# Conv branch of a decoder layer: one 512-column product for the high weights, a bank for each unit

## The chip, the cores and the metric

The kernel runs on one core of one Trainium2 chip. The metric is the device time of one execution in microseconds; the time of a kernel is the median of its runs.

## The reference

One decoder layer on 256 tokens of width 1024, in float32: gated token mixers in parallel, then a feed-forward block, each followed by a LayerNorm. Cut to what matters here:

```python
proj = x @ w_in          # q | k | v | B | C | h | gates, 1024 -> 5120 columns
q, k = apply_partial_rope(q, cos, sin), apply_partial_rope(k, cos, sin)
y_att = moba_attention(q, k, v) @ w_attn_out       # 256 tokens: one block, plain causal attention
y_cnv = (gate_b * causal_dwconv(gate_c * h_in, conv_w_mix)) @ w_conv_out
mix = (g_att * y_att + g_cnv * y_cnv) @ w_o
x = layer_norm(DEEPNORM_ALPHA * x + mix, ln1_g, ln1_b)
u = causal_dwconv(x @ w_up, conv_w_ffn)
f = (silu(u[..., :D_FF]) * u[..., D_FF:]) @ w_down
x = layer_norm(DEEPNORM_ALPHA * x + f, ln2_g, ln2_b)
```

B, C and h have 512 columns each (the conv branch); the gates have 2048.

## The kernel before

**Products in three passes.** To keep float32 accuracy, every operand is split into a high part (rounded to the format that TensorE multiplies) and a low part (the rest). A product is then high x high, high x low and low x high, summed in PSUM. x is kept split and transposed in `xT`, eight k-tiles of 128 rows, each with 256 high columns and then 256 low columns (`xh` and `xl` are views of them). Weights come by DMA as raw chunks of 1 MB, two *units* of work in each, through three buffers (`RAW_BUFS`), queued on SP. `split` makes the high part `wh` on ScalarE and the low part `wl` on VectorE (`hl_split`, L213 to L215); nine buffers of each hold them (`HL_BUFS`).

**Units and steps.** A unit of the conv branch or of the gates is 128 output columns of `w_in`: eight k-tiles of 128x128 weights. The order of the conv units is h, c, b for the first 256 channels (`pr` 0) and then for the second (`pr` 1), two units each (`e` 0 and 1), twelve in all; sixteen gate units follow. Each unit is a step: `ahead(u)` queues the splits up to unit u+4 (`LA`), then TensorE's products are queued, then `run(u)` queues what was put down for that step with `at`. Every engine works off its queue in this order. Counted from the first h unit as step 0 (`C0`), attention is put down beside the conv units for each pair of heads p: `scores` at step 4+3p, `masked` (row maxima, VectorE) one step later, `exps` (ScalarE) two and `normalize` (VectorE) three steps later; `probs_T` at step 9+4p, the splits of the transposed probabilities `probs_hl` at 10+4p and 11+4p, `attend` at 12+4p, and `attend_hl` (from the bank of `attend` into `aT`, ScalarE and VectorE) at 13+4p.

**PSUM.** There are eight banks: four in the pool `acc` (the projections) and four in the pool `ps` (scores, transposes, attention outputs), each handed out in turn. A bank is handed out again once all that read it is done.

**Two forms of a unit.** `unit_cols` (L305 to L313) takes for each k-tile three products of 256 columns: wh with xh, wh with xl, wl with xh, all into the same 256 columns of a bank. The conv units use it, and the two units of one name share a bank, 256 columns each. `unit_cols_wide` (L315 to L323) takes for each k-tile one product of wh with all 512 columns of `xT` (L321), and afterwards eight products of wl with the high columns into the first half of the bank (L323). The gates use it: the two halves of a gate's bank are added by `gate_sum` (ScalarE copies one half to SBUF in L577, VectorE adds the other in L578).

**The conv work.** `conv1` copies h out of its bank (L532, ScalarE) and multiplies c from its bank with it (L535, VectorE); `conv2` applies the three taps (L542 on ScalarE, L545 four times on VectorE); `conv3` multiplies b from its bank (L551) and splits the result into `yT`, which is used after the gates. They stand at the first b unit of their `pr`, one and two steps later. `scratch` hands out SBUF buffers of one tag in turn, six of them.

Of the kernel before, what the change touches and what calls it, by code (L numbers as in the profile page):

```python
# [12 lines left out]
AF = mybir.ActivationFunctionType  # L13
ALU = mybir.AluOpType

P = 128
S = 256
# [35 lines left out]
OFF_B, OFF_C, OFF_H, OFF_G = 3 * AW, 3 * AW + CW, 3 * AW + 2 * CW, 3 * AW + 3 * CW  # L53
# [84 lines left out]
def layer_kernel(ctx: ExitStack, tc: tile.TileContext, x, wpack, cpack, ln1_g, ln1_b, ln2_g, ln2_b, out):  # L138
    nc = tc.nc
# [10 lines left out]
    def acc_bank(name):  # L150
        return psum.tile([P, 512], F32, tag="acc", name=name)

    def ps_bank(name):
        return ps_pool.tile([P, 512], F32, tag="ps", name=name)

    def scratch(shape, name, bufs=None, tag="scr"):
        return tmp.tile(shape, F32, tag=tag, name=name, bufs=bufs or 6)
# [5 lines left out]
    chunks, plan_units, U = plan()  # L163
# [49 lines left out]
    def hl_split(h, l, src, eng=None):  # L213
        nc.scalar.activation(h, src, AF.Copy)  # L214
        (eng or nc.vector).tensor_tensor(l, src, h.bitcast(F32), op=ALU.subtract)  # L215
# [38 lines left out]
    xT = big.tile([P, KT, 2, S], F32R, tag="xT", name="xT")  # L254
    xh, xl = xT[:, :, 0], xT[:, :, 1]
# [49 lines left out]
    def unit_cols(u, o, bh, bl, n0=0):  # L305

        un = units[u]
        nk = un["shape"][0]
        for k in range(nk):
            wh, wl = un["h"][:, k, n0:n0 + P], un["l"][:, k, n0:n0 + P]  # L310
            nc.tensor.matmul(o, wh, bh[:, k, :], start=k == 0, stop=False)  # L311
            nc.tensor.matmul(o, wh, bl[:, k, :], start=False, stop=False)  # L312
            nc.tensor.matmul(o, wl, bh[:, k, :], start=False, stop=k == nk - 1)  # L313

    def unit_cols_wide(u, bank, b):  # L315


        un = units[u]
        nk = un["h"].shape[1]
        for k in range(nk):  # L320
            nc.tensor.matmul(bank, un["h"][:, k, :], b[:, k].rearrange("p a s -> p (a s)"), start=k == 0, stop=False)  # L321
        for k in range(nk):
            nc.tensor.matmul(bank[:, 0:S], un["l"][:, k, :], b[:, k, 0], start=False, stop=k == nk - 1)  # L323
# [4 lines left out]
    def ahead(u):  # L328
        for v in range(cur["u"], u + LA + 1):
            split(v)  # L330
        cur["u"] = max(cur["u"], u + LA + 1)
# [102 lines left out]
    def at(u, f, *a):  # L434
        after.setdefault(u, []).append((f, a))

    def run(u):
        for f, a in after.pop(u, []):
            f(*a)
# [14 lines left out]
    for p in range(4):  # L454
        s = C0 + 4 + 3 * p
# [4 lines left out]
        s = C0 + 9 + 4 * p  # L460
# [66 lines left out]

    CB = {}

    def conv1(pr):  # L530
        h = scratch([P, 2, S], f"ch{pr}")
        nc.scalar.activation(h, CB["h", pr], AF.Copy)  # L532
        z = scratch([P, 2, S + 2], f"z{pr}", tag="z", bufs=1)
        nc.vector.memset(z[:, :, 0:2], 0.0)
        nc.vector.tensor_tensor(z[:, :, 2:S + 2], CB["c", pr], h, op=ALU.mult)  # L535
        CB["z", pr] = z

    def conv2(pr):
# [9 lines left out]

    def conv3(pr):
        t = CB["t", pr]  # L550
        nc.vector.tensor_tensor(t, CB["b", pr], t, op=ALU.mult)  # L551
        hl_split(yT[:, 0, 2 * pr:2 * pr + 2, :], yT[:, 1, 2 * pr:2 * pr + 2, :], t)

    for pr in range(2):
        at(U[(OFF_B, pr)], conv1, pr)
        at(U[(OFF_B, pr)] + 1, conv2, pr)
        at(U[(OFF_B, pr)] + 2, conv3, pr)
        for nm, off in (("h", OFF_H), ("c", OFF_C), ("b", OFF_B)):
            bank = acc_bank(f"{nm}{pr}")
            CB[nm, pr] = bank.rearrange("p (e t) -> p e t", e=2)  # L560
            for e in range(2):
                u = U[(off, pr)] + e
                ahead(u)
                unit_cols(u, bank[:, e * 256:(e + 1) * 256], xh, xl)
                run(u)


# [16 lines left out]
    for j in range(16):  # L584
        u = U[("g", 0)] + j
# [27 lines left out]
    for half in range(2):  # L613
        for e in range(2):
            ua, uc = U[("ao", half)] + e, U[("co", half)] + e
            for n in range(2):
# [4 lines left out]
                bank = ps_bank(f"y{i}")  # L621
# [327 lines left out]
```

## Time and profile before

| | |
|---|---|
| median of 3 runs | 370.72 us (370.24 to 373.15) |
| the profiled execution, its own time | 370.11 us |
| its span in the profile | 368.3 us |
| granted TensorE clock, mean | 0.993 |
| TensorE busy | 359.3 us, 2122 products |
| VectorE busy | 291.9 us |
| ScalarE busy | 218.5 us |
| stage of the conv units | 37.75 to 77.89 us |
| stage of the gate units | 77.89 to about 129 us |

The profile is of one execution. Times are from the start of its span in microseconds; the span leaves out some 2 us of the execution's time. Engines: PE is TensorE's product, PEld its weight load, DVE is VectorE, ACT is ScalarE. A row of a timeline has the start, the duration, the engine, the line of the kernel, the operation, `out<-in` and the shapes, and in brackets the idle time just before it and what ended that. Products are pipelined, so their durations overlap, and the distance from one start to the next is what a product costs. A row of a group has the count, the busy time, the mean duration of one in ns, and the idle time before them. A line can be that of a helper: most splits stand under L214 and L215.

### The profile page before, as it was taken

Reading aid. Unit: us, or ns where it says so; the run is one execution under the profiler, and the core shown is the slowest. Engines: PE = TensorE matmul, PEld = TensorE weight load, DVE = VectorE, ACT = ScalarE, POOL = GpSimd, SP = SyncE. Lnnn points to the kernel's source line nnn. Section 1 sums busy time; section 2 is a strip of 40 time slices with the busy share of each in tenths; the row PEclk is TensorE's granted clock in tenths of the full one; section 3 lists DMA queues with packets and bytes.
Section 4 is the critical chain, followed back from the end, with each engine's and each line's share of the span. In section 5 each row is a group of like instructions: output and inputs, shape, how many; then the busy total and the mean of one; then the engine's idle time right before and its main releaser. Section 6 shows DMA issues by size and latency. Waiting matters only on the chain.

```text
span 368.3 us, 5515 instructions
## 1 busy us (share of the span) xinstructions
PE 359.3 (98%) x2122; PEld 317.3 (86%) x2122; DVE 291.9 (79%) x499; ACT 218.5 (59%) x365; POOL 9.3 (3%) x27
## 2 busy tenths in 40 slices
PE   8999999999999999999999999999999999999991
PEld 8888999998888899988888888888888888888891
DVE  4786968788586579869759898987888697899784
ACT  3766568568787645634266676675666566576300
POOL 2000000000000000102100000000000000000012
PEclk9999999999999999999999999999999999999997
DMA  7959653633555554586250935448274545562011
GB/s 273 332 210 356 216 222 116 230 114 116 229 201 164 207 197 169 187 362 222 122 219 12 340 122 223 163 182 322 65 299 132 212 149 204 219 235 109 1 57 57
DMA packets 11385, 69.63 MB, mean 189 GB/s; under 512 B 1248, under 2 KB 1888, under 8 KB 4320
## 3 DMA queue, kind: packets, MB, share of 16 engines
q1 hardware_dynamic: 10784, 67.20, 49.9%
q0 software_dynamic: 576, 2.10, 1.7%
q8 instruction: 16, 0.26, 0.3%
q14 instruction: 9, 0.07, 0.1%
HBM read 68.24 MB, written 1.05 MB: 188 GB/s over the span
## 4 chain that ended last, share of the span: by engine, by line
PE 98%; DVE 1%; issue 0%; DVEq 0%
PE pb L321 20%; PE pb L323 10%; PE g L321 8%; PE d L292 5%; PE d L293 5%; PE d L294 5%; PE g L323 4%; PE q L493 3%; PE k L493 3%; PE v L493 3%; PE y L313 2%; PE y L312 2%; PE y L311 2%; PE o L293 2%; PE o L292 2%; PE o L294 2%
## 5 line engine op out<-in xcount | busy, mean ns | idle before, releaser
L215 DVE TENSOR_TENSOR wl<-raw,wh 128x1024 fp32r<-128x1024 f32 (+1 forms) x70 | 77.0, 1123 | 16.6 <-ACT wh L214 16.0
L197 DVE TENSOR_TENSOR wl<-raw,wh 128x1024 fp32r<-128x1024 f32 x58 | 70.8, 1222 | 16.3 <-ACT wh L192 15.7
L321 PE MATMUL pb<-x1T,wh 128*128 128x512 f32 x320 | 79.8, 391 | 0.0
L214 ACT ACTIVATE wh<-raw 128x1024 fp32r<-128x1024 f32 (+1 forms) x70 | 66.1, 973 | 16.6 <-DMA raw<-in_wpack 11.0
L192 ACT ACTIVATE wh<-raw 128x1024 fp32r<-128x1024 f32 x58 | 60.9, 1054 | 18.5 <-DMA raw<-in_wpack 18.4
L321 PEld LDWEIGHTS pb<-x1T,wh 128*128 128x128 f32 x320 | 58.5, 188 | 11.1
L323 PEld LDWEIGHTS pb<-x1T,wl 128*128 128x128 f32 x320 | 43.7, 190 | 3.1
L323 PE MATMUL pb<-x1T,wl 128*128 128x256 f32 x320 | 44.6, 282 | 0.0
L321 PE MATMUL g<-xT,wh 128*128 128x512 f32 x128 | 32.3, 394 | 0.0
L292 PE MATMUL d<-wh,f 128*128 128x512 f32 x80 | 31.3, 391 | 0.0
L293 PE MATMUL d<-wl,f 128*128 128x512 f32 x80 | 31.3, 391 | 0.0
L294 PE MATMUL d<-wh,f 128*128 128x512 f32 x80 | 31.1, 389 | 0.0
L321 PEld LDWEIGHTS g<-xT,wh 128*128 128x128 f32 x128 | 23.0, 189 | 4.2
L709 ACT ACTIVATE fb<-pb 128x512 f32<-128x512 f32 x20 | 11.9, 596 | 24.5 <-PE pb L323 23.9
L727 DVE SCALAR_TENSOR_TENSOR fc<-fb,consts,fc 128x254 f32<-128x254 f32 x40 | 19.4, 484 | 1.4
L725 DVE SCALAR_TENSOR_TENSOR fc<-fb,consts,fc 128x255 f32<-128x255 f32 x40 | 19.2, 479 | 0.0
L323 PEld LDWEIGHTS g<-xT,wl 128*128 128x128 f32 x128 | 17.5, 190 | 1.3
L719 ACT ACTIVATE fc<-fb,consts 128x256 f32<-128x256 f32 x40 | 18.0, 497 | 0.3 <-DVE fb L713 0.3
L713 DVE TENSOR_TENSOR fb<-pb,fb 128x512 f32<-128x512 f32 x20 | 13.8, 688 | 5.4 <-ACT fb L709 5.1
L323 PE MATMUL g<-xT,wl 128*128 128x256 f32 x128 | 17.9, 282 | 0.0
L294 PEld LDWEIGHTS d<-wh,f 128*128 128x128 f32 x80 | 15.0, 188 | 3.2
L292 PEld LDWEIGHTS d<-wh,f 128*128 128x128 f32 x80 | 15.1, 188 | 2.7
(184 smaller groups left out, 676.6 us busy)
## 6 DMA issues: line engine op xcount, KB each, us to landing
raw<-in_wpack SPq DMA_DIRECT2D x55, 1024.0 KB, 4.9
raw<-in_wpack SPq DMA_DIRECT2D x6, 896.0 KB, 6.1
xr<-in_x SPq DMA_DIRECT2D x1, 1024.0 KB, 7.0
ln<-in_ln_g POOLq DMA_DIRECT2D x2, 512.0 KB, 5.4
ln<-in_ln_b POOLq DMA_DIRECT2D x2, 512.0 KB, 6.0
raw<-in_wpack SPq DMA_DIRECT2D x3, 256.0 KB, 3.1
raw<-in_wpack SPq DMA_DIRECT2D x1, 512.0 KB, 6.0
out<-x SPq DMA_DIRECT2D x2, 256.0 KB, 2.0
```

What stands on the lines that cost most here:

```text
L192: nc.scalar.activation(units[u]["h"], raw_of(u), AF.Copy)
L197: nc.vector.tensor_tensor(units[u]["l"], raw_of(u), units[u]["h"].bitcast(F32), op=ALU.subtract)
L214: nc.scalar.activation(h, src, AF.Copy)
L215: (eng or nc.vector).tensor_tensor(l, src, h.bitcast(F32), op=ALU.subtract)
L292: nc.tensor.matmul(o, ah, bh, start=start, stop=False)
L293: nc.tensor.matmul(o, ah, bl, start=False, stop=False)
L294: nc.tensor.matmul(o, al, bh, start=False, stop=stop)
L321: nc.tensor.matmul(bank, un["h"][:, k, :], b[:, k].rearrange("p a s -> p (a s)"), start=k == 0, stop=False)
L323: nc.tensor.matmul(bank[:, 0:S], un["l"][:, k, :], b[:, k, 0], start=False, stop=k == nk - 1)
L493: nc.tensor.matmul(banks[m][t], (xl if p == 2 else xh)[:, k, t * P:(t + 1) * P], wl if p == 1 else wh, start=k == 0 and p == 0, stop=k == ...
L725: nc.vector.scalar_tensor_tensor(c[:, 1:S], pb[:, a * S:a * S + S - 1], w_ffn(1, j), c[:, 1:S], op0=ALU.mult, op1=ALU.add)
L727: nc.vector.scalar_tensor_tensor(c[:, 2:S], pb[:, a * S:a * S + S - 2], w_ffn(0, j), c[:, 2:S], op0=ALU.mult, op1=ALU.add)
```

## The change

The conv units take the wide form, and each has a bank of its own, so that twelve banks are handed out in this stage where six were. A new function `conv_sum` adds the halves of a bank on the way out, into an SBUF tile that two units of a name share; it stands one step after its unit. `conv1` and `conv3` read h, c and b from these tiles, the copy of h in `conv1` is gone, and `conv1`, `conv2` and `conv3` stand one step later than before.

```diff
+    def conv_sum(nm, pr, e):
+
+        if e == 0:
+            CB["s", nm, pr] = scratch([P, 2, S], f"c{nm}{pr}")
+        s = CB["s", nm, pr][:, e]
+        bank = CB.pop((nm, pr, e))
+        nc.scalar.activation(s, bank[:, S:2 * S], AF.Copy)
+        nc.vector.tensor_tensor(s, bank[:, 0:S], s, op=ALU.add)
+
     def conv1(pr):
-        h = scratch([P, 2, S], f"ch{pr}")
-        nc.scalar.activation(h, CB["h", pr], AF.Copy)
         z = scratch([P, 2, S + 2], f"z{pr}", tag="z", bufs=1)
         nc.vector.memset(z[:, :, 0:2], 0.0)
-        nc.vector.tensor_tensor(z[:, :, 2:S + 2], CB["c", pr], h, op=ALU.mult)
+        nc.vector.tensor_tensor(z[:, :, 2:S + 2], CB["s", "c", pr], CB["s", "h", pr], op=ALU.mult)
         CB["z", pr] = z
...
-        nc.vector.tensor_tensor(t, CB["b", pr], t, op=ALU.mult)
+        nc.vector.tensor_tensor(t, CB["s", "b", pr], t, op=ALU.mult)
         hl_split(yT[:, 0, 2 * pr:2 * pr + 2, :], yT[:, 1, 2 * pr:2 * pr + 2, :], t)
 
     for pr in range(2):
-        at(U[(OFF_B, pr)], conv1, pr)
-        at(U[(OFF_B, pr)] + 1, conv2, pr)
-        at(U[(OFF_B, pr)] + 2, conv3, pr)
         for nm, off in (("h", OFF_H), ("c", OFF_C), ("b", OFF_B)):
-            bank = acc_bank(f"{nm}{pr}")
-            CB[nm, pr] = bank.rearrange("p (e t) -> p e t", e=2)
+            for e in range(2):
+                at(U[(off, pr)] + e + 1, conv_sum, nm, pr, e)
+        at(U[(OFF_B, pr)] + 1, conv1, pr)
+        at(U[(OFF_B, pr)] + 2, conv2, pr)
+        at(U[(OFF_B, pr)] + 3, conv3, pr)
+        for nm, off in (("h", OFF_H), ("c", OFF_C), ("b", OFF_B)):
             for e in range(2):
                 u = U[(off, pr)] + e
                 ahead(u)
-                unit_cols(u, bank[:, e * 256:(e + 1) * 256], xh, xl)
+                CB[nm, pr, e] = acc_bank(f"{nm}{pr}{e}")
+                unit_cols_wide(u, CB[nm, pr, e], xT)
                 run(u)
```

## The prediction

> **What bounds the kernel now.** I read the page first, then busy time by stage, then the timelines of TensorE, VectorE and ScalarE around the conv units, and last the groups kept apart by shape.
>
> ```profile
> span 368.3 us, 5515 instructions
> ...
> PE 359.3 (98%) x2122; PEld 317.3 (86%) x2122; DVE 291.9 (79%) x499; ACT 218.5 (59%) x365; POOL 9.3 (3%) x27
> ...
> PE 98%; DVE 1%; issue 0%; DVEq 0%
> ```
>
> The last row is the chain of work that ended last: 98% of it is TensorE following itself. Whatever shortens TensorE's stream shortens the kernel, unless another engine then ends last somewhere. For the stage of the change:
>
> ```profile
> 37.50:77.80 40.30, 40.30 (x348) 39.43 (x347) 33.41 (x79) 26.45 (x51) 0.00 (x0) 1.00 0.53 186
> ```
>
> The columns are span, PE, PEld, DVE, ACT, POOL, clock, DMA. TensorE never pauses here, its weight loads fill 39.43 of 40.30 us, the granted clock is 1.00. VectorE is busy 33.41 us: 6.9 us of slack in the stage, not spread evenly. So there are two questions: how much shorter does TensorE's stream get, and does the added work on VectorE and ScalarE stay hidden.
>
> **TensorE's term.** A conv unit is 24 products of 256 columns, each with its own weight load. A gate unit already has the new form: 8 products of 512 columns, then 8 of 256.
>
> ```profile
> 57.81 0.28 PE L311 MATMUL h<-xT,wh 128*128 128x256 f32 x1
> ...
> 60.69 0.28 PE L311 MATMUL h<-xT,wh 128*128 128x256 f32 x1
> ...
> 81.74 1.99 PE L321 MATMUL g<-xT,wh 128*128 128x512 f32 x8
> 83.57 1.12 PE L323 MATMUL g<-xT,wl 128*128 128x256 f32 x8
> 84.52 0.27 PE L409 MATMUL ptp<-ident,sm 128*128 128x128 f32 x1
> ...
> 85.27 0.95 PE L374 MATMUL s<-qkT 64*128 64x128 f32 x12
> ```
>
> Durations overlap, so starts count. Conv unit 6 (I number units and steps from the first h unit, 0) runs from 57.81 to the start of unit 7 at 60.69: 2.88 us, 120 ns for each product. Gate unit 13 runs from 81.74 to the transposes at 84.52: 2.78 us, of which the wide part is 1.83 (229 ns each) and the narrow part 0.95 (119 ns each). Two narrow products cost 240 ns and one wide 229: 11 ns for each of 8 k-tiles, 0.09 to 0.10 us for a unit. Twelve units: 96 products and 96 weight loads fewer, and **1.2 us less on TensorE**. Both forms are measured at the same clock with the same xT, so the term's bounds are narrow: 1.1 to 1.2 us. The instruction count falls by 192, the product time only by 3%, since as many columns stream as before.
>
> The Trainium skill speaks against even that much. Its page "TensorE: Matmul & The Clock Gate" (Back-to-back issue gap) gives a warm matmul N/2.4 + 2.5 ns: 109 ns for 256 columns, 216 for 512, so that pairing two saves 2.5 ns only. An estimate by that page: 96 x 2.5 ns = 0.24 us. The trace does not agree: 120 and 229 ns, a saving of 11 ns.
>
> **Added on ScalarE and VectorE.** Each unit gets one copy out of the bank on ScalarE and one add on VectorE. The same two exist for the gates; the copy of h (L532) goes away.
>
> ```profile
> L578 DVE TENSOR_TENSOR gs<-g,gs 128x256 f32<-128x256 f32 x16 | 6.7, 422 | 8.2 <-ACT gs L577 8.1
> ...
> L577 ACT ACTIVATE gs<-g 128x256 f32<-128x256 f32 x16 | 6.1, 383 | 5.9 <-PE g L323 5.8
> ...
> L215 DVE TENSOR_TENSOR yT<-ct,yT 128x512 fp32r<-128x512 f32 x2 | 1.4, 692 | 1.4 <-ACT yT L214 1.4
> ...
> L551 DVE TENSOR_TENSOR ct<-b,ct 128x512 f32<-128x512 f32 x2 | 1.4, 686 | 0.0
> ...
> L532 ACT ACTIVATE ch<-h 128x512 f32<-128x512 f32 x2 | 1.2, 596 | 0.0
> ```
>
> VectorE: 12 x 0.422 = 5.1 us at most; neighbouring instructions overlap by about 0.08 us in these timelines (wl below: 1.23 long, next start after 1.14), so about 0.35 each, 4.2 us. ScalarE: 12 x 0.383 - 1.2 = 3.4 us at most. The products with c and b stay, now from SBUF; I cost that at nothing, because 128x512 lasts the same from either: L551 reads b from a bank in 686 ns, L215 on ct reads SBUF alone in 692. conv1, conv2 and conv3 move one step later; their DVE and ACT instructions issue no DMA. No unit and no transfer is reordered.
>
> **Bank reuse.** Twelve banks rotate through four. Unit u+4 needs the sum of unit u, which is queued in step u+1, so three units of TensorE (over 8 us) lie between. In the order worked out below the closest is the sum of unit 6, done near 65.9, against unit 10 starting near 70. Cost: nothing, cover about 4 us; if the cover were gone each missing us would be a us of TensorE.
>
> **Where VectorE's delay meets TensorE.** The s bank of scores(3), second half, is the bank of attend(0) (four ps banks in turn), and attend_hl(0) must empty it. Both stand in step 13, with VectorE's order ahead of it crowded:
>
> ```profile
> 52.82 1.23 DVE L215 TENSOR_TENSOR wl<-raw,wh 128x1024 fp32r<-128x1024 f32 x1
> ...
> 67.03 1.22 DVE L215 TENSOR_TENSOR wl<-raw,wh 128x1024 fp32r<-128x1024 f32 x1
> 70.00 1.23 DVE L215 TENSOR_TENSOR wl<-raw,wh 128x1024 fp32r<-128x1024 f32 x1 [1.76 <-ACT wh L214]
> 71.46 0.56 DVE L215 TENSOR_TENSOR vpt<-ptp,vpt 128x384 fp32r<-128x384 f32 x1 [0.23 <-ACT vpt L214]
> 71.94 0.17 DVE L399 RECIPROCAL st<-st 128x4 f32<-128x4 f32 x1
> ...
> 73.07 0.69 DVE L535 TENSOR_TENSOR z<-c,ch 128x512 f32<-128x512 f32 x1
> ...
> 73.67 1.22 DVE L215 TENSOR_TENSOR wl<-raw,wh 128x1024 fp32r<-128x1024 f32 x1
> 74.81 0.56 DVE L215 TENSOR_TENSOR vpt<-ptp,vpt 128x384 fp32r<-128x384 f32 x1
> 75.27 0.28 DVE L382 CUSTOM_DVE_ANT_0 sm<-s,mask 128x128 f32<-128x128 f32 x1
> ...
> 76.58 1.92 DVE L545 SCALAR_TENSOR_TENSOR ct<-z,consts,ct 128x256 f32<-128x256 f32 x4
> 78.41 1.22 DVE L215 TENSOR_TENSOR wl<-raw,wh 128x1024 fp32r<-128x1024 f32 x1
> 79.55 0.69 DVE L551 TENSOR_TENSOR ct<-b,ct 128x512 f32<-128x512 f32 x1
> ...
> 81.88 1.23 DVE L215 TENSOR_TENSOR wl<-raw,wh 128x1024 fp32r<-128x1024 f32 x1 [0.26 <-ACT wh L214]
> 83.03 0.41 DVE L215 TENSOR_TENSOR aT<-av,aT 64x256 fp32r<-64x256 f32 x1
> 83.88 0.43 DVE L215 TENSOR_TENSOR aT<-av,aT 64x256 fp32r<-64x256 f32 x1 [0.45 <-ACT aT L214]
> ```
>
> And ScalarE, whose exps wait for VectorE's row maxima and stand ahead of copies that VectorE waits for:
>
> ```profile
> 67.16 0.40 ACT L393 ACTIVATE sm<-sm,st 128x128 f32<-128x128 f32 x1 [2.98 <-DVE st L385]
> ...
> 68.93 1.04 ACT L214 ACTIVATE wh<-raw 128x1024 fp32r<-128x1024 f32 x1
> ```
>
> From start to start these rows give: wl 1.14, vpt 0.47, normalize 1.13, z 0.60, masks 1.31, four taps 1.83, conv3 to the next step 2.0 with its wait for yT, exps 1.77, the two aT 1.28 (83.03 to 84.31). Before, attend_hl(0) ends at 84.31 and scores(3) starts at 85.27: 0.96 us to spare.
>
> I lay the new order into these prices from the wl of step 4, at 52.8. Step 4: wl, sum to 54.3. Step 5: wl, masks to 56.75, sum, z to 57.7. Step 6: wl to 58.85; the sum waits for its copy behind exps(0) (56.75 to 58.55, then 0.4) and ends at 59.3; the taps end at 61.25. Step 7: wl, normalize(0) to 63.5, conv3 to 65.5, sum to 65.9. Step 8: wl (its wh is late, behind yT) to 67.25, masks to 68.55, sum to 68.9. Step 9: wl to 70.0; exps(1) until 70.4, copy, sum at 71.15. Step 10: wh behind that copy, wl to 72.9, vpt, normalize(1) to 74.5, sum to 74.85. Step 11: wl, vpt to 76.45, masks to 77.75, sum, z to 78.7. Step 12: wl to 79.85; exps(2) until 79.65, copy, sum at 80.3, taps to 82.2. Step 13: wl to 83.35, the two aT to 84.65.
>
> So only 0.35 us of the 4.2 shows at that place: conv2 and conv3 moved behind it by a step each, and old waits (1.76 at 70.00) are partly filled. TensorE, 1.2 us ahead by then, reaches scores(3) at 85.27 - 1.2 = 84.07 and **waits about 0.6 us** there. What is queued behind it is all of TensorE's stream, so the wait counts in full. **Sum: -1.2 + 0.6 = -0.6 us.** Bounds: with every sum at its full 0.42 us, aT ends about 1 us later (wait 1.6, net +0.4); where ScalarE's waits swallow more, there is no wait (net -1.2).
>
> What is late next: conv3(1) and the first gate sums now follow in step 13, and attend(1) needs the last vpt:
>
> ```profile
> 91.77 0.55 DVE L215 TENSOR_TENSOR vpt<-ptp,vpt 128x384 fp32r<-128x384 f32 x1
> 94.64 0.40 PE L292 MATMUL av<-vpt 128*128 128x512 f32 x1
> ```
>
> Vpt is there at 92.3, TensorE comes at 94.64: 2.3 us to spare. ScalarE's step 14 begins some 2 us later than before, so this lands within 0.3 us of TensorE; I take 0. Later steps have one wl and one sum on VectorE for 2.8 us of TensorE, and the lag goes. The wl leads are far: wl of unit 16 ends near 79.85, unit 16 starts after 90.
>
> **How the span becomes the time.** The profiled execution took 370.11 us for its span of 368.3; less 0.6 that is 369.5. The median of the runs, 370.72, is 0.6 above it and one of its three stands at 373.15, so from the median the sum gives 370.1. I predict between them: **369.8 us**.
>
> **The rivals.** (a) All is hidden: the full 1.2 us, 368.9 from the profiled time to 369.5 from the median, 369.2. For it: 6.9 us of VectorE slack against 4.2 added. Against: the slack was VectorE waiting for ScalarE, and the new copies lengthen just that loop. (b) Slower: VectorE's lag at attend_hl(0). The place is scores(3), it decides once attend_hl(0) ends more than 0.96 us later than before (after 85.27), and each us beyond costs one. If of the 4.2 us nothing fell into old waits and nothing moved behind, it would end at 88.5, TensorE loses 88.5 - 85.27 = 3.2 us and the time is 373.6; with half of that lag (2.1 us) it ends at 86.4, 1.1 us slower, 371.5. Against: the order laid out above. (c) The wide products bring nothing here: a wide one costs what two narrow ones cost, scores(3) then comes at 85.27, later than 84.65, no wait, 370.4. Against: 229 to 240 ns in the rows. The skill's gap formula, named above, would nearly be this case, 0.24 us faster. (d) The banks do run out: more than 4 us of delay at the sums of units 6 to 8, some 4 us for TensorE, 374.5; only the lag of (b) in full gets there.
>
> **Chances.** Forecast (-1.0 to 0) 0.45; (a) 0.20; (b) up to 3.2 us 0.23; (c) 0.06; (d) 0.06. The range runs from 368.9, the full gain on the profiled time, to 371.9, which takes in half of (b) and the scatter of the runs. The forecast's own range is 369.1 to 370.5. A measurement of this kernel can tell about 1% (3.7 us) from no change; nothing reaches a gain of that size (0.02), the ends of (b) and (d) reach the loss (0.08), the rest is within it (0.90).
>
> **What would show it.** Right: 16 products for a conv unit, units of 2.78 us, TensorE's start of unit 12 about 1.2 us earlier than 77.89, sums of about 420 ns and copies of about 380 at the new lines, and scores(3) starting near 84.7, just after an aT on VectorE, with the gate units from then on 0.6 us earlier than before. Wrong: units of 2.88 us (the product term), scores(3) straight after the transposes (the wait), or later than 85.27 (rival b), or a pause ahead of a conv unit whose bank waits for a sum (rival d).

## The result: slower, by a wait at a later place than the two that the prediction checked

The changed kernel takes 373.01 us (median of 6, 372.04 to 374.31) against 370.62 us before (median of 6): ratio 1.0063, 95% interval 1.004 to 1.0086. The forecast was 0.6 us faster, the range ended at 371.9. The lines of the page after that answer to those of before:

```profile
span 370.8 us, 5343 instructions
...
PE 359.9 (97%) x2026; PEld 313.0 (84%) x2026; DVE 295.9 (80%) x511; ACT 220.0 (59%) x375; POOL 9.3 (2%) x27
...
PE 82%; DVE 10%; ACT 6%; issue 1%; DVEq 0%; ACTq 0%
```

TensorE has 96 products fewer, as worked out. But the chain that ended last no longer runs through TensorE alone: 16% of the span lie on VectorE and ScalarE. Who waited, from the waits of TensorE in the profile after (of before only the first row exists):

```profile
PE warm L229 <- DVE zeros L219: 1.0, 1, 1.0
PE av L293 <- DVE vpt L215: 0.9, 1, 0.9
PE av L292 <- ACT vpt L214: 0.8, 1, 0.8
PE s L374 <- DVE aT L215: 0.2, 1, 0.2
```

The timeline of TensorE after, by starts:

```profile
38.25 1.98 PE L321 MATMUL h<-xT,wh 128*128 128x512 f32 x8
40.07 1.11 PE L323 MATMUL h<-xT,wl 128*128 128x256 f32 x8
41.02 2.00 PE L321 MATMUL h<-xT,wh 128*128 128x512 f32 x8
...
84.80 0.32 PE L374 MATMUL s<-qkT 64*128 64x128 f32 x1
86.18 2.12 PE L321 MATMUL g<-xT,wh 128*128 128x512 f32 x8
...
106.74 1.11 PE L323 MATMUL g<-xT,wl 128*128 128x256 f32 x8
108.67 0.49 PE L292 MATMUL av<-vpt 128*128 128x512 f32 x1 [0.82 <-ACT vpt L214]
110.01 0.50 PE L293 MATMUL av<-vpt 128*128 128x512 f32 x1 [0.85 <-DVE vpt L215]
```

This execution reached its first conv product 0.50 us later than the one before (38.25 against 37.75), ahead of all that was changed, so I count from there. A unit takes 2.77 us (38.25 to 41.02). Scores(3) is reached after 46.55 us in place of 47.52: 0.97 us gained. It then takes 1.38 us to the next unit (84.80 to 86.18) in place of 0.88: the 0.5 us of wait that was forecast. What was not forecast is attend(2), step 20: the unit ahead of it ends near 107.69 (106.74 + 0.95), and the second product of attend(2) starts at 110.01 in place of 107.92.

What comes too late there is the last vpt. The lines of before for that place, from the timelines of VectorE, TensorE and ScalarE:

```profile
106.85 0.55 DVE L215 TENSOR_TENSOR vpt<-ptp,vpt 128x384 fp32r<-128x384 f32 x1
```

```profile
107.50 0.40 PE L292 MATMUL av<-vpt 128*128 128x512 f32 x1
```

```profile
86.45 1.28 ACT L572 ACT_TABLE_LOAD   x1
87.75 0.91 ACT L572 ACTIVATE gates<-gs,consts 128x256 f32<-128x256 f32 x2
89.26 0.39 ACT L577 ACTIVATE gs<-g 128x256 f32<-128x256 f32 x1 [0.60 <-PE g L323]
```

Vpt was done at 107.40 and TensorE came at 107.50: 0.1 us to spare. And of after, the same engines, VectorE first:

```profile
86.35 0.69 DVE L558 TENSOR_TENSOR ct<-cb,ct 128x512 f32<-128x512 f32 x1
87.74 0.69 DVE L215 TENSOR_TENSOR yT<-ct,yT 128x512 fp32r<-128x512 f32 x1 [0.70 <-ACT yT L214]
...
98.84 0.42 DVE L587 TENSOR_TENSOR gs<-g,gs 128x256 f32<-128x256 f32 x1 [3.96 <-ACT gs L586]
...
109.41 0.55 DVE L215 TENSOR_TENSOR vpt<-ptp,vpt 128x384 fp32r<-128x384 f32 x1
```

```profile
87.07 0.63 ACT L214 ACTIVATE yT<-ct 128x512 fp32r<-128x512 f32 x1 [2.35 <-DVE ct L558]
...
89.73 1.28 ACT L581 ACT_TABLE_LOAD   x1
...
91.84 0.36 ACT L586 ACTIVATE gs<-g 128x256 f32<-128x256 f32 x1
...
93.55 1.28 ACT L393 ACT_TABLE_LOAD   x1
...
96.73 1.28 ACT L581 ACT_TABLE_LOAD   x1
...
103.97 0.38 ACT L214 ACTIVATE aT<-av 64x256 fp32r<-64x256 f32 x1 [2.33 <-DVE aT L215]
```

Conv3 now stands in step 13, so ScalarE idles 2.35 us for its product and starts the first sigmoids' table load at 51.48 us from the first conv product, in place of 48.70. From there to attend(2) the long rests of the two engines are waits for each other, and they are as long as before: VectorE waits 3.96 us for ScalarE (98.84; at 96.28 before), whose work has three table loads of 1.28 us in it, as before, and ScalarE waits 2.33 us for VectorE (103.97; 2.34 at 101.41 before). In such a wait a lag can't go, since the engine waited for is late too. It could go where ScalarE waited for TensorE, 0.60 us at 89.26; after, that copy (91.84) waits for nothing. The lag arrives at the last vpt as 2.06 us (71.16 from the first conv product, in place of 69.10). The chain in order of time (start, duration, engine, tile, line) shows the same. It leaves TensorE at the second transposes of q and k, and comes back at attend(2):

```profile
50.44 0.45 PE qkt L359 x4
```

```profile
110.01 0.50 PE av L293
```

All pieces between the two are VectorE's, ScalarE's or their issue.

### The profile page after: what moved, and what is told of

The parts are those of the page before. It is cut to its first block, busy times and chain, and to the rows that moved or that the text cites. A ratio compares the mean times of both kernels' runs of the same rounds, so it can differ in the third digit from the quotient of the medians.

```text
span 370.8 us, 5343 instructions
## 1 busy us (share of the span) xinstructions
PE 359.9 (97%) x2026; PEld 313.0 (84%) x2026; DVE 295.9 (80%) x511; ACT 220.0 (59%) x375; POOL 9.3 (2%) x27
## 3 DMA queue, kind: packets, MB, share of 16 engines
HBM read 68.24 MB, written 1.05 MB: 187 GB/s over the span
## 4 chain that ended last, share of the span: by engine, by line
PE 82%; DVE 10%; ACT 6%; issue 1%; DVEq 0%; ACTq 0%
PE pb L321 20%; PE pb L323 10%; PE d L292 5%; PE d L293 5%; PE d L294 5%; PE g L321 3%; DVE wl L215 3%; PE q L493 3%; PE k L493 3%; PE v L493 3%; PE y L313 2%; PE y L312 2%; PE y L311 2%; PE o L292 2%; PE o L294 2%; PE o L293 2%
```

## The experiments

Theory A: from step 4 on VectorE and ScalarE, each in order and each waiting for the other, are the bound up to attend(2), and the added sums with conv3 in step 13 made that loop longer than TensorE's stream. Beside the medians I use the time from the first conv product to the first product behind the gates (y), since the executions' start-up scatters (37.75 to 39.68 us). Each of these times is from the profile of one execution:

| kernel | median us (before, beside it) | first conv product to y, us |
|---|---|---|
| before | | 92.03 |
| changed | 373.01 (370.62) | 93.95 |
| wide products alone | 369.97 (370.74) | 91.03 |
| narrow products, sums | 374.07 (370.74); again 373.95 (370.76) | 94.22; 94.23 |
| changed again | 374.10 (370.76) | 95.47 |
| conv1 to conv3 at their old steps | 374.07 (370.74) | 95.38 |
| conv3 of the second half late | 370.00 (370.74) | 91.57 |
| conv1 to conv3 of it late | 369.62 (370.76) | 91.08 |
| first sigmoids late | 371.28 (370.76) | 92.24 |
| no adds | 372.33 (370.71) | 93.30 |
| no copies | 371.47 (370.71) | 92.66 |
| wait filled with products | 372.48 (370.71) | 93.92 |
| before, first sigmoids late | 370.94 (370.71) | 92.03 |

**The wide products alone**, in the kernel before:

```diff
-                unit_cols(u, bank[:, e * 256:(e + 1) * 256], xh, xl)
+                unit_cols_wide(u, bank, xT)
```

> The kernel before with the conv units' products in the wide form and nothing else: the two units of a name still share a bank and conv1 and conv3 read it as before, with no copy and no add (so the two parts of a unit are not added, and the first unit of a name is overwritten by the second; the products, their count and their order are the change's). Theory A (the delay comes from VectorE and ScalarE work that reaches attend(2), step 20, late; in the profile of before its last vpt ended at 107.40 and attend(2) started at 107.50, so there was 0.1 us to spare): units of 2.78 us, TensorE 1.0 us ahead at step 12, and the same 1.0 us lost again as a wait at attend(2), near 107.5. Net 0: 370.3 to 370.9. Rival B (the wide form or its banks cost time on TensorE itself): 372 to 373. Rival C (TensorE sets the time throughout, only the sums cost): the full gain, 369.3 to 369.7.

Ratio 0.9979 (0.9964 to 0.9994), the stage 1.00 us shorter, no wait on TensorE. The median lies between the ranges of theory A and rival C, 0.3 us from either; the stage has the full gain, as rival C had it. Rival B falls: the form gains. Of theory A one part falls too: attend(2) did not eat the gain. Before, ScalarE's copy at 89.26 waits for TensorE (0.60 us, above), so there the loop is let go by TensorE and moves forward with it. With the wide products alone that copy waits 0.60 us again, and the 0.1 us to spare moves along: the last vpt ends at 106.55, attend(2) starts at 106.65. The loop is a bound of its own only where it lags too far for that copy to wait, as after the change.

**Narrow products with the banks, sums and steps of the change.**

```diff
-                unit_cols_wide(u, CB[nm, pr, e], xT)
+                unit_narrow(u, CB[nm, pr, e])   # k-tile 0 wide; then wh x xh and wl x xh into
+                                                # columns 0:256, wh x xl into 256:512
```

> The changed kernel with its banks, sums and moved steps, but three products of 256 columns for each k-tile (wh with xl goes into the second half of the bank; only the first k-tile is wide). Theory A: the chain that ends at attend(2) from about 74 us on has no product in it, so it comes as late as in the changed kernel and TensorE just waits about 1 us less; time 372.6 to 373.4, as the changed kernel. Rival B: without the wide products the loss goes, 370.4 to 371. Rival C (the costs simply add: the loss of TensorE's 1.0 us on top): 373.8 to 374.4.

374.07, in the range of rival C. But from the first conv product the second product of attend(2) came at 72.04 us, in the changed kernel at 71.76, so the two were run side by side.

> The changed kernel itself, to stand beside the next one on the same chip: 372.6 to 373.4.

> The changed kernel with narrow products once more, beside the changed kernel. In its first profile attend(2) comes 72.0 us after the first conv product, in that of the changed kernel 71.8, so the chain is as long; but its median was 1.1 us above, of which 1.2 us in the profile lay ahead of the first conv product, where the kernels are alike. Theory A: beside the changed kernel it is 0 to 0.5 us slower. Rival C (the costs add up): 1.0 to 1.2 us slower.

374.10 for the changed kernel and 373.95 for this one. The medians settle less than they seem to. The changed kernel itself went from 373.01 to 374.10 by a fall of the granted clock, which is taken up below; it is in five of its six executions here, and in two of the six with narrow products. For the comparison I take profiles of executions without that fall, the first of the changed kernel and the second of this one. TensorE is 0.86 us later at scores(3) (47.41 from the first conv product, in place of 46.55), and the stage is only 0.28 us longer (94.23 against 93.95). At the second transposes of q and k, where the chain leaves TensorE, it is 0.31 us later (12.33 against 12.02), and the second product of attend(2) comes 0.29 us later (72.05 against 71.76). So the slower products ahead of that point show in the time, and those of the eight units behind it don't, as theory A has it; by the stage rival C falls. The wait at attend(2) did not get shorter, since the chain came later too; what went is the wait at scores(3). Without the fall of the clock the executions of this kernel still took about 1 us more than those of the changed one (372.95 to 374.38 against 372.04 to 372.63). In the profiles all but 0.3 us of that lies ahead of the first conv product (39.68 and 39.23 against 38.25 and 38.14), where the work is the same; why is open.

**conv1 to conv3 at their old steps.**

```diff
-        at(U[(OFF_B, pr)] + 1, conv1, pr)
-        at(U[(OFF_B, pr)] + 2, conv2, pr)
-        at(U[(OFF_B, pr)] + 3, conv3, pr)
+        at(U[(OFF_B, pr)], conv1, pr)
+        at(U[(OFF_B, pr)] + 1, conv2, pr)
+        at(U[(OFF_B, pr)] + 2, conv3, pr)
```

> The changed kernel with conv1, conv2 and conv3 at their old steps (each one step earlier than in the changed kernel; the sums stay where they are). Theory A: all of this work still stands ahead of attend(2) on VectorE and ScalarE, so moving it by a step changes little: 372.2 to 373.2. Rival D (the loss comes from the move of conv1 to conv3 by a step, not from the added sums): the gain comes back, 369.5 to 370.3.

Ratio 1.0091 (1.0074 to 1.0107). Neither expectation: not better, as rival D had it, but worse than theory A said too. The waits of TensorE in its profile:

```profile
PE s L374 <- DVE aT L215: 2.5, 1, 2.5
PE warm L229 <- DVE zeros L219: 1.0, 1, 1.0
```

With conv3 ahead of attend_hl(0), all of the lag shows at scores(3) as one wait of 2.5 us, and behind it attend(2) waits no more. So the move of conv3 to step 13 shifts the place of the wait, and the lag is there either way. That the time is worse than theory A said has another cause, in the granted clock (the third number from the right) by windows behind the wait, which ends at 87.34:

```profile
84.50:87.30 2.80, 0.33 (x2) 0.18 (x1) 2.07 (x5) 1.42 (x5) 0.00 (x0) 1.00 0.18 23
87.30:90.00 2.70, 2.66 (x15) 2.17 (x16) 2.63 (x8) 2.46 (x4) 0.00 (x0) 0.61 0.83 337
90.00:93.00 3.00, 3.00 (x16) 2.58 (x15) 2.10 (x11) 1.34 (x4) 0.00 (x0) 0.78 0.09 33
93.00:96.00 3.00, 3.00 (x19) 2.62 (x18) 2.12 (x3) 2.97 (x5) 0.00 (x0) 1.00 0.00 0
```

The wide part of the next unit takes 3.29 us (88.38 to 91.67) in place of 1.95 in the changed kernel, and the scores' products 1.04 in place of 0.85, together 1.5 us. Without them the stage would be 93.9 us long (an estimate, 95.38 less 1.5), as long as the changed kernel's. The times of whole executions can't confirm it: four of the five have a mean clock of 0.990 or 0.991, and the fifth, at 0.994, took 374.04 us.

**conv3 of the second 256 channels late.** Their tiles lie in the buffer of q and k, because six scratch buffers would not last that long.

```diff
-        at(U[(OFF_B, pr)] + 3, conv3, pr)
+        at(U[(OFF_B, pr)] + (3, 12)[pr], conv3, pr)
...
-            CB["s", nm, pr] = scratch([P, 2, S], f"c{nm}{pr}")
+            CB["s", nm, pr] = scratch([P, 2, S], f"c{nm}{pr}") if pr == 0 else in_qk("hcb".index(nm))
```

> The changed kernel with conv3 of the second 256 channels at step 22, behind attend(2), in place of step 13; the conv tiles of these channels lie in the buffer of q and k, which is free by then, in place of scratch. Theory A: conv3 took VectorE and ScalarE from 86.35 to 88.43 in the profile after, a link of the chain; without it the chain is 2.1 us shorter, attend(2)'s wait falls from about 2.2 us to 0 to 0.3, and the time falls by about 2: 370.6 to 371.3. The wait of about 0.5 us at scores(3), which stands ahead of conv3, stays. Rival B: no change, 372.6 to 373.4.

370.00, ratio 0.9982 (0.9968 to 0.9995), somewhat better than expected: the wait at attend(2) is gone altogether, that at scores(3) stays. All twelve sums are still there. So conv3's 2.1 us on the two engines, at that place, is what turns the change from a gain into a loss. The move of the tiles is a rival here, since the changed kernel might have waited for scratch buffers. Its profile shows no such wait: from 52 us to attend(2) ScalarE waits only for row maxima, for conv3's product and for attend_hl's aT, and VectorE only for ScalarE's part of a split or a sum.

**All of conv1 to conv3 of that half late**, steps 21 to 23:

```diff
-        at(U[(OFF_B, pr)] + 1, conv1, pr)
-        at(U[(OFF_B, pr)] + 2, conv2, pr)
-        at(U[(OFF_B, pr)] + 3, conv3, pr)
+        at(U[(OFF_B, pr)] + (1, 11)[pr], conv1, pr)
+        at(U[(OFF_B, pr)] + (2, 12)[pr], conv2, pr)
+        at(U[(OFF_B, pr)] + (3, 13)[pr], conv3, pr)
```

> The changed kernel with all of conv1, conv2 and conv3 of the second 256 channels behind attend(2), at steps 21, 22 and 23 in place of 11, 12 and 13; their tiles lie in the buffer of q and k. The sums stay. Theory A (VectorE and ScalarE, in order and waiting for each other, are the bound from about step 4 to attend(2); TensorE has no spare there): z, four taps and the two copies for them leave the chain besides conv3, some 2.5 us ahead of attend_hl(0), so the wait at scores(3) goes too and the full 1.0 us of TensorE is kept: 369.4 to 369.9. Rival B (the form or the banks cost time): above 370.7.

369.62, ratio 0.9976 (0.996 to 0.9991), and of TensorE's waits only the one at the very start is left. Scores(3) goes through at once. This version beats both kernels; its stage is 0.95 us shorter than before, which is the whole of TensorE's term.

**The first sigmoids behind exps(3)**, two table loads fewer:

```diff
-        at(U[("g", 0)] + max(j + 1, 2), gate, j)
+        at(U[("g", 0)] + max(j + 1, 3), gate, j)
```

> The changed kernel with the first two gates' sigmoids one step later, behind exps(3), so that ScalarE loads its table once in place of three times between steps 14 and 15 (two loads of 1.28 us fewer). Theory A: these loads are links of the chain (89.73, 93.55 and 96.73 in the profile after); 2.6 us fewer takes away the wait of some 2 us at attend(2); the wait of 0.5 us at scores(3), which stands ahead of them, stays: 370.1 to 370.6. Rival E (VectorE alone is the bound, by its busy time): no change, 372.6 to 373.4.

371.28, ratio 1.0008 (0.9993 to 1.0024): most of the loss is back, so table loads on ScalarE are links of the chain and rival E falls. But the stage got 1.7 us shorter (93.95 to 92.24) where 2.6 were taken out, and the time stayed 0.7 us above the range. The timeline of ScalarE shows why:

```profile
93.29 0.40 ACT L393 ACTIVATE sm<-sm,st 128x128 f32<-128x128 f32 x1 [1.08 <-DVE st L385]
```

Relieved of 2.6 us, ScalarE waits 1.08 us for VectorE's row maxima. The same edit in the kernel before, as a control:

> The kernel before with the first two sigmoids behind exps(3), as a control: two table loads fewer on ScalarE. Theory A: before the change TensorE waits nowhere in this stage, so nothing is gained: 370.2 to 371.2.

370.94, ratio 1.0005 (0.9987 to 1.0023): nothing, as TensorE waits nowhere in this stage.

**The two halves of a sum.** Without the adds:

```diff
         nc.scalar.activation(s, bank[:, S:2 * S], AF.Copy)
-        nc.vector.tensor_tensor(s, bank[:, 0:S], s, op=ALU.add)
```

> The changed kernel without the twelve adds on VectorE (the conv branch then takes only the half of each bank that ScalarE copies). Theory A, with VectorE's 4.2 us in the chain: the waits at scores(3) and attend(2) go, TensorE keeps its 1.0 us: 369.4 to 370.0. Rival G (ScalarE's copies, which stand behind exps and ahead of the next wh, are what lengthens the chain): above 371.5.

Without the copies:

```diff
-        nc.scalar.activation(s, bank[:, S:2 * S], AF.Copy)
-        nc.vector.tensor_tensor(s, bank[:, 0:S], s, op=ALU.add)
+        nc.vector.tensor_tensor(s, bank[:, 0:S], xl[:, 0, :].bitcast(F32), op=ALU.add)
```

> The changed kernel without the twelve copies on ScalarE; VectorE's add takes a piece of x in place of the copied half. Theory A: the adds keep their 4.2 us, but none waits for ScalarE's exps any more (some 0.3 us each at the sums of steps 6, 9 and 12, and 0.3 for each wh behind a copy): 370.2 to 371.5, part of the waits stays. Rival G: 369.4 to 370.0.

372.33 (ratio 1.0045, 1.0027 to 1.0064) and 371.47 (1.0014, 0.9999 to 1.0029). The first is in rival G's range, the second in theory A's. The first contradicts theory A's size: 4.2 us of VectorE's work taken away shorten the stage by 0.65 us only. The waits in its profile are those of the changed kernel, less the one at scores(3):

```profile
PE av L293 <- DVE vpt L215: 0.9, 1, 0.9
PE av L292 <- ACT vpt L214: 0.8, 1, 0.8
```

The adds of steps 6, 9 and 12 stand in the shadow of ScalarE's exps, and without them VectorE waits for ScalarE instead (0.86 us at the taps, 59.45 and 80.17, where it had not waited, and 2.02 at the wl of step 10 in place of 0.74 and 0.52). The copies cost more (1.3 us of the stage), though not all, as rival G had it. Neither engine's work alone is the chain; it changes sides where one waits for the other, and taking work from one side gives back only what the other side doesn't hold. With either half gone, conv3 in step 13 still stands where it hurts.

**The wait filled with products.** In the twelve executions of the changed kernel (the first six and the six of the second time) the times fall into two groups by the mean granted clock: 372.04 to 372.63 us at 0.992 to 0.996 (four), 373.39 to 374.55 us at 0.988 or 0.989 (eight). The profile of the changed kernel shown above is of the first kind, that of the second time is of the other. In it, busy time by windows behind attend(2):

```profile
95.00:110.00 15.00, 13.33 (x77) 11.37 (x77) 9.26 (x18) 12.59 (x28) 0.00 (x0) 1.00 0.57 211
110.00:113.00 3.00, 3.00 (x11) 2.44 (x12) 2.74 (x4) 2.08 (x5) 0.00 (x0) 0.62 0.82 287
113.00:116.00 3.00, 3.00 (x19) 2.77 (x18) 1.09 (x4) 1.48 (x4) 0.00 (x0) 0.82 0.67 232
116.00:125.00 9.00, 9.00 (x52) 7.85 (x51) 5.84 (x9) 5.89 (x12) 0.00 (x0) 1.00 0.42 152
```

The third number from the right, the granted clock, is 0.62 and 0.82 for six us behind the wait, which costs 1.5 us (95.47 against 93.95 for the stage). In the other profile it is 1.00 throughout. The test:

```diff
         b = ps_bank(f"av{p}")
+        if p == 2:
+            for i in range(30):
+                nc.tensor.matmul(b[:, 0:P], zeros, zeros, start=True, stop=True)
```

> The changed kernel with 30 products of zeros (128x128, bf16) queued on TensorE ahead of attend(2), into attend(2)'s own bank, which its first product clears: they fill the wait with TensorE work. Theory F: of 12 timed or profiled executions of the changed kernel the 8 with a mean granted clock of 0.988 or 0.989 took 373.4 to 374.6, the 4 with 0.992 to 0.996 took 372.0 to 372.6, and in one profile of the former the clock falls to 0.62 right behind the wait at attend(2); with the wait filled the clock stays and every execution takes 372.0 to 372.9. Rival H (the clock falls for some other reason): still 373.4 and more in half of the executions.

372.48, ratio 1.0042 (1.0028 to 1.0055); eleven executions from 372.00 to 373.54, not one with a clock under 0.992. Rival H falls. Theory F holds for the clock: it stays up, the 30 products lie in the wait, and the stage is as long as without the drop (93.92). Its range for the times, up to 372.9, was too narrow: 372.96 and 373.54 lie above it, so the times scatter without the clock too.

## Why the prediction was wrong

Point by point, by its own steps.

- **TensorE's term** (1.1 to 1.2 us): 0.97 to 1.00 us measured, units of 2.77 to 2.79 us. Right in kind, a little large. The estimate by the Trainium skill's gap formula (0.24 us) is a quarter of it.
- **The sums' prices** (422 and 383 ns): right, the adds took 418 to 422 ns and the copies 378 to 380. VectorE's busy time rose by 4.0 us (291.9 to 295.9), 4.2 forecast; ScalarE's by 1.5 (218.5 to 220.0), 3.4 forecast at most.
- **Bank reuse** at nothing: right, no conv unit waits for its bank.
- **The wait at scores(3)**: 0.6 us forecast, 0.5 measured. Laid out by hand, attend_hl(0) ended at 84.65; it ended at 85.18 in an execution that was 0.50 us late. This part of the order was right, and not by errors that cancel: the other times laid out ahead of it, moved by 0.50, are within 0.2 us of VectorE's timeline after.
- **The step that failed** is "What is late next". It said that the lag of some 2 us at ScalarE's step 14 "goes", because later steps have one wl and one sum on VectorE. The lag was there (2.78 us at the table load), but I counted VectorE's work alone. The two engines are one loop, whose long rests are waits for each other, so the lag does not go in them; 0.7 us of it went, 0.60 of that where ScalarE had waited for TensorE. And I checked attend(1), with 2.3 us to spare, and not attend(2), which had 0.1. There 2.06 us of lag arrived, and TensorE came 0.3 us earlier (69.44 from the first conv product, in place of 69.75): 2.06 + 0.3 - 0.1 is about the 2.2 us that it waited. The rows for this (107.40 and 107.50, and the waits of the two engines) stood in the trace of before. The 0.1 us alone would have told too little, since with the wide products alone it moved along with TensorE. From unit to unit, attend(2) took 3.25 us (107.69 to 110.94) in place of 1.05, attend(1) 0.13 more than before: 0.97 gained, less 0.50, 0.13 and 2.20, is the loss of 1.9 us in the stage.
- **Rival (b)** had the mechanism, VectorE's lag behind the sums, and put it at scores(3). With conv3 at its old step that is what happens (2.5 us there). As the change orders it, conv3 comes behind attend_hl(0) and the lag meets TensorE seven steps later.
- **The clock** was in no rival: in the changed kernel the wait has a second price, 1.5 to 1.7 us, in two executions of three. Without it the loss is still there: 372.48 us with the wait filled, beyond the range's end of 371.9.

## What to carry to other kernels

A stream that never waits can be one tenth of a us from waiting: before work is added beside it, follow the added lag through every later place where the two meet, not to the next one, and look up the spare time of each. Two engines that take turns have a common length that neither busy time shows; taking 4.2 us from one gave 0.65 us, while moving 2.1 us that nobody needed soon out of the loop gave back all. If work must be added to such a loop, move out of it what is used last (here conv3, whose result is needed after the gates).

## What the runs showed of the hardware

In the profile of the changed kernel's second time, two waits of TensorE of 0.81 and 0.86 us, with one product between them, were followed by a granted clock of 0.62 and 0.82 over six us. With conv1 to conv3 at their old steps, one wait of 2.51 us was followed by 0.61 and 0.78 over 5.7 us. By the mean clock (0.988 to 0.990 in place of 0.992 and more) it happened in 8 of 12 executions of the changed kernel and in 6 of 12 with narrow products. Without the adds, with waits of 0.79 and 0.85 us in the profile, it happened in 2 of 12; without the copies, with 0.20 and 0.84, in none of 12. Filled with products of zeros it did so in none of 11. The Trainium skill's page "TensorE: Matmul & The Clock Gate" (Part 1: The HAM clock gate) has the clock fall after at least one idle window of about 3.4 us, the windows running freely. That the same wait lowers the clock in some executions and not in others would fit windows that run freely; that so short a wait is enough does not fit the page, and the measurement decides.
